# Two-layer encoder trunk on one core: first loads in another order, plain float32 behind three LayerNorms, gates at other points

## The chip, the cores and the metric

The kernel runs on 1 core of one Trainium2 chip. The metric is the device time of one execution in microseconds, median of the runs shown. Engines are named as in the profile: PE is TensorE (matmul), PEld its weight load, DVE is VectorE, ACT is ScalarE, POOL is GpSimd, SP is SyncE, which issues nearly all of this kernel's loads.

## The reference, cut to what matters

x is (1, 256, 1024) in float32; there are two layers, and LayerNorm sits behind every residual sum. The modulation of every sub-layer comes from one condition vector through a 1024 x 6144 matrix per layer.

```python
cond = jax.nn.silu(c)
for l in range(DEPTH):
    mod = (cond @ ada_w[l] + ada_b[l])[:, None, :]
    sh_m, sc_m, g_m, sh_f, sc_f, g_f = jnp.split(mod, 6, axis=-1)
    h = x * (1.0 + sc_m) + sh_m
    if l % 2 == 0:
        y = even_mixer(h, ...)            # pooling mixer | windowed attention, one in- and one out-projection
    else:
        y = spatial_gating_mixer(h, ...)  # gelu(h @ w_in) -> u, v; v normed, mixed over 128 positions; (u*v) @ w_out
    x = layer_norm(ALPHA * x + (1.0 + g_m) * y, ln_g[l, 0], ln_b[l, 0])
    h = x * (1.0 + sc_f) + sh_f
    if l % 2 == 0:
        y = swiglu(h, ...)                # 1024 -> 2816 -> 1024
    else:
        y = moe_swiglu(h, ...)            # router, top 2 of 8 experts, 1024 -> 3584 -> 1024 each
    x = layer_norm(ALPHA * x + (1.0 + g_f) * y, ln_g[l, 1], ln_b[l, 1])
```

The kernel works to float32 accuracy.

## The kernel before, in words

The 256 positions are two tiles of 128 (`t` = 0, 1); the 1024 channels are eight blocks of 128 (`KD`, index `kk`). Nothing is scheduled by a tool: each engine runs its instructions in the order in which the program writes them, and an instruction that waits holds up all behind it on its engine.

**Weights.** The class `Stream` (`st`) brings all weights in one fixed order, as pieces of 512 KB ("halves"), on the queue of SP, into a pool of 34 slots (`wtile`). `st.step()` takes the next half: a piece of the condition matrix goes through one DVE multiply-and-sum (`add_ada`, L270; the text calls it an ada step), a weight half is split into two reduced-float32 parts, `hi` by an ACT copy (L193) and `lo` by a DVE subtraction (L194), unless it is marked `RAW`. A split weight is multiplied by `mm3`: three reduced-float32 matmuls, hi x hh, lo x hh, hi x hl (L363 to L365), where `hh`, `hl` are the two parts of the activations. A RAW one is multiplied in plain float32. `st.advance(n)` takes n steps at that place in the program, `st.get()` takes steps until the halves asked for are there. `ROOM` is how many slots the loader leaves free.

**Start.** The condition vector (`cond`) and the small columns (`colt`) are loaded from ACT's queue, all else from SP's. For each `kk` in turn DVE does two ada steps (scale and shift) and `h` (L551), PE the in-projection in plain float32 (L561 to L571), and for the first four `kk` DVE makes one group of `band`, the pooling matrix (L513, L514). `cn` and the two `band` tiles take slots of the weights' pool.

**Attention.** `attend(0)` (tile 0: transposes L639, copies L641, matmuls L650), then `out_rows` (L717, plain float32, y = [pooled | attention] x w_out, 16 records of 128x512 per two `kk`), `attended` puts the heads' result behind (L664). DVE forms `o` (L656) between.

**Gates.** When all eight ada steps of a gate are made, `gate` puts it on all partitions by eight matmuls (L281) and two ACT copies; `st.finish` and `st.flush` say where.

**The three norms** (`norm_modulate`): DVE sums the residual and takes statistics, POOL the root, ACT (tile 0) or DVE (tile 1) normalises (`z`, L790, L797), PE transposes (L768), ACT or DVE apply scale and shift (`hf`), then `hh` and `hl` are made, and the first product behind the norm follows: gate and up of the first FFN block after norm 1 (`gu_tile`), `v` of the gating mixer after norm 2 (`v_half`), router logits and the dense first half of expert 0 after norm 3 (`logits`, `dense`).

**The rest**, FFN blocks, gating mixer and the experts, runs through `mm3` at one long stretch each.

Of the kernel before, what the change touches and what calls it, by code (L numbers as in the profile page):

```python
# [21 lines left out]
P = 128  # L22
# [29 lines left out]
def trunk_(es, tc, stream, experts, blocks, x, xT, c, columns, ada_w, ln_g, ln_b, ev_w_in, pool_w, ev_sink, ev_w_out,  # L52
# [51 lines left out]
    class Stream:  # L104
# [103 lines left out]
        def ensure(self, i):  # L208

            while self.made < i:  # L210
                self.step()
            self.flush()
# [21 lines left out]
        def get(self):  # L234
# [4 lines left out]
            for i in unit:  # L239
# [5 lines left out]
                if self.halves[i] == RAW:  # L245
                    for kk in range(part.shape[1]):
                        yield part[:, kk, :]
                    self.live -= 1
# [61 lines left out]
    for g in range(NFB // 2 + 1):  # L310
        if g < NFB // 2:
            for i, w in enumerate((ffn_w_gate, ffn_w_up)):
                st.add(cols(w[0], g * 256, 256))
                for _ in range(ADA[g]):
                    add_ada(*rest.pop(0))
# [3 lines left out]
    for nh in range(2):  # L319
        for k0 in (0, 4):  # L320
            st.add(cols(od_w_in[0], D + nh * 512, 512, k0, 4))
# [9 lines left out]
    def expert_units(stage, step):  # L331
# [111 lines left out]
    with ExitStack() as ph:  # L443
# [12 lines left out]
        A.dma_start(cond, c.to_broadcast([P, D]))  # L456
# [39 lines left out]
        cn = wtile(F32, "cn").rearrange("p (g n) -> p g n", g=4)  # L496
# [11 lines left out]
        band = [wtile(F32, "band").rearrange("p (g t n) -> p g t n", g=2, t=2) for _ in range(2)]  # L508

        def make_band(g):  # L510
            for t in range(NT):
                b = band[g // 2][:, g % 2, t, :]
# [27 lines left out]
        for t in range(NT):  # L540
            nc.sync.dma_start(xt[t], x[0, t * P:(t + 1) * P, :])
# [42 lines left out]
        st.ROOM = 15  # L584
# [109 lines left out]
        for g in range(4):  # L694
            psg.append(bank())
            for t in range(NT):
                T.matmul(psg[g][:, 0:S], lhsT=pt[:, t, g * P:(g + 1) * P], rhs=band[g // 2][:, g % 2, t, :],
# [11 lines left out]
        st.advance(2)  # L709
# [10 lines left out]
        o = [attend(0, V.tensor_copy, 1)]  # L720
# [16 lines left out]
        st.advance(4)  # L737
        out_rows(range(4, KD), (1,))

        def keep_warm(n):  # L740

            ps = psa.tile([P, 512], F32, tag="a", name="idle")
            for _ in range(n):
                T.matmul(ps[:, 0:P], lhsT=ones, rhs=ident, start=True, stop=True)

        def norm_modulate(y, gt, mods, then, keep=None, after=lambda: None):

            hh, hl = (big([P, KD, S], F32R, name=n) for n in ("hh", "hl"))  # L750
            then = then((hh, hl))
            z = [t4.tile([P, D], F32, tag="z", name="z", bufs=2) for _ in range(NT)]

# [17 lines left out]
            def affine(tp, t, q, eng):  # L771
                sa, sb = mods
                sl = slice(q * 4, q * 4 + 4), slice(t * P, (t + 1) * P)
                hf = keep[:, sl[0], sl[1]] if keep is not None else hp.tile([P, 4, P], F32, tag="hf", name="hf")
                for k in range(4):
                    kk = q * 4 + k
                    if eng is V:
                        V.tensor_scalar(hf[:, k, :], tp[:, k, :], sa[:, kk:kk + 1], sb[:, kk:kk + 1],
                                        op0=ALU.mult, op1=ALU.add)
                    else:  # L780
                        A.activation(hf[:, k, :], tp[:, k, :], AF.Identity, scale=sa[:, kk:kk + 1], bias=sb[:, kk:kk + 1])
                A.activation(hh[:, sl[0], sl[1]], hf, AF.Copy)
                return lambda: V.tensor_tensor(hl[:, sl[0], sl[1]], hf, hh[:, sl[0], sl[1]], op=ALU.subtract)
# [8 lines left out]
            lows = [affine(tp, 0, q, A) for q, tp in enumerate(tps)]  # L792
            next(then)
# [736 lines left out]
```

## Time and profile before

| what | value |
|---|---|
| time, median of 3 runs | 1343.64 us (1342.23 to 1344.15) |
| the profiled execution | 1340.86 us, span 1339.0 us |
| PE busy | 1284.6 us (96%) |
| DVE busy | 941.3 us (70%) |
| ACT busy | 679.3 us (51%) |
| DMA | 470.46 MB, mean 351 GB/s over the span |
| granted TensorE clock, mean | 0.982 of full speed |

Times inside the kernel are microseconds from the span's start. Idle time of PE stands in brackets in the rows of a timeline, with what it waited for. A plain float32 matmul shows as two records, a reduced-float32 one as one. Rows of a timeline merge like instructions in a row; a row's duration contains the tail of its last record, so the pace is better read from the start of a row to the start of the next.

### The profile page before, as it was taken

The numbers are of one execution on the slowest core, as the hardware profiler recorded it, in microseconds if no ns is written. First come the engines' busy times: TensorE is split into PE (matmuls) and PEld (weight loads), VectorE is DVE, ScalarE is ACT, GpSimd is POOL, SyncE is SP. The second block draws the span as 40 slices with busy tenths as digits, with TensorE's granted clock in tenths as the row PEclk, the third lists the DMA queues.
The fourth block names the chain that finished last, engine by engine and source line by source line (L and its number), as shares of the span: only waits on it lengthen the run. The fifth ranks groups of instructions, "written<-read, shape, count | busy, mean of one in ns | idle before, by whom it ended". The sixth has DMA issues, their size and how long they took to land. (4 is left out here: it accounts for less than half of the span.)

```text
span 1339.0 us, 19237 instructions
## 1 busy us (share of the span) xinstructions
PE 1284.6 (96%) x6468; PEld 945.1 (71%) x6468; DVE 941.3 (70%) x1162; ACT 679.3 (51%) x860; POOL 17.1 (1%) x73
## 2 busy tenths in 40 slices
PE   4987999998999999999999999999999999999995
PEld 3664999997888688644678888864467888886342
DVE  5696799986886888530798899753069899976303
ACT  0224444444625777421777777742167787774200
POOL 1001000000000000000000000000000000000001
PEclk9988999999999999999999999999999999999998
DMA  9995589997396589999999999899999999999993
GB/s 372 409 409 220 211 323 338 366 349 293 116 345 236 205 322 324 386 409 408 409 409 409 409 409 386 318 381 409 409 409 409 409 409 409 360 326 375 409 409 142
DMA packets 129579, 470.46 MB, mean 351 GB/s; under 512 B 14520, under 2 KB 14656, under 8 KB 129472
## 3 DMA queue, kind: packets, MB, share of 16 engines
q1 hardware_dynamic: 128880, 468.25, 90.7%
q8 instruction: 52, 0.85, 0.3%
q10 hardware_dynamic: 592, 0.91, 0.2%
q14 instruction: 55, 0.45, 0.1%
HBM read 468.05 MB, written 1.05 MB: 350 GB/s over the span
## 5 line engine op out<-in xcount | busy, mean ns | idle before, releaser
L194 DVE TENSOR_TENSOR lo<-raw,hi 128x1024 fp32r<-128x1024 f32 x506 | 604.5, 1220 | 118.0 <-ACT hi L193 93.4
L193 ACT ACTIVATE hi<-raw 128x1024 fp32r<-128x1024 f32 x506 | 514.9, 1054 | 147.0 <-PE y L364 17.0
L270 DVE CUSTOM_DVE_ANT_0 raw<-raw,cond,colt 128x1024 f32<-128x1024 f32 x96 | 118.5, 1278 | 0.0
L363 PE MATMUL pg<-hi,hh 128*128 128x512 f32 x288 | 117.3, 407 | 0.0
L364 PE MATMUL pg<-lo,hh 128*128 128x512 f32 x288 | 114.2, 397 | 0.7 <-DVE lo L194 0.7
L365 PE MATMUL pg<-hi,hl 128*128 128x512 f32 x288 | 114.0, 396 | 0.0
L364 PE MATMUL pu<-lo,hh 128*128 128x512 f32 x280 | 111.3, 397 | 1.2 <-DVE lo L194 1.2
L363 PE MATMUL y<-hi,ah 128*128 128x512 f32 x280 | 112.3, 401 | 0.0
L365 PE MATMUL y<-hi,al 128*128 128x512 f32 x280 | 111.0, 397 | 1.1 <-DVE al L1196 1.1
L363 PE MATMUL pu<-hi,hh 128*128 128x512 f32 x280 | 111.5, 398 | 0.0
L365 PE MATMUL pu<-hi,hl 128*128 128x512 f32 x280 | 111.0, 396 | 0.0
L364 PE MATMUL y<-lo,ah 128*128 128x512 f32 x280 | 110.9, 396 | 0.0
L1404 DVE TENSOR_TENSOR act<-act,pu 128x512 f32<-128x512 f32 (+1 forms) x47 | 31.2, 664 | 101.0 <-PE pu L1178 92.4
L1194 ACT ACTIVATE ah<-psT 128x512 fp32r<-128x512 f32 (+2 forms) x47 | 27.2, 578 | 132.6 <-PE psT L1189 132.2
L363 PE MATMUL psgu<-hh,hi 128*128 128x256 f32 x320 | 90.1, 282 | 0.0
L365 PE MATMUL psgu<-hh,lo 128*128 128x256 f32 x320 | 90.1, 281 | 0.0
L364 PE MATMUL psgu<-hl,hi 128*128 128x256 f32 x320 | 89.6, 280 | 0.0
L1178 PE MATMUL pu<-raw,hs 128*64 128x512 f32 (+1 forms) x384 | 76.6, 542 | 0.0
L1178 PE MATMUL pg<-raw,hs 128*64 128x512 f32 (+1 forms) x384 | 75.8, 542 | 0.0
L1402 ACT ACTIVATE act<-pg 128x512 f32<-128x512 f32 (+1 forms) x47 | 27.4, 584 | 84.1 <-PE pg L1178 62.3
L1210 PE MATMUL y<-raw,ah 128*64 128x512 f32 x288 | 65.5, 597 | 0.0
L363 PEld LDWEIGHTS pg<-hi,hh 128*128 128x128 f32 x288 | 54.2, 188 | 14.7 <-ACT hi L193 2.4
(281 smaller groups left out, 1872.2 us busy)
## 6 DMA issues: line engine op xcount, KB each, us to landing
raw<-in_experts SPq DMA_DIRECT2D x668, 512.0 KB, 10.1
raw<-in_stream SPq DMA_DIRECT2D x204, 512.0 KB, 7.3
lng<-in_ln_g SPq DMA_DIRECT2D x4, 512.0 KB, 6.7
lnb<-in_ln_b SPq DMA_DIRECT2D x4, 512.0 KB, 6.6
xT<-in_xT SPq DMA_DIRECT2D x2, 512.0 KB, 7.2
x<-in_x SPq DMA_DIRECT2D x2, 512.0 KB, 10.6
guest<-in_experts SPq DMA_DIRECT2D x2, 512.0 KB, 10.5
guests<-in_experts SPq DMA_DIRECT2D x2, 512.0 KB, 7.0
```

Of the source, the lines that this page charges most:

```text
L193: A.activation(hi, raw, AF.Copy)
L194: V.tensor_tensor(lo, raw, hi, op=ALU.subtract)
L270: V.tensor_tensor_reduce(raw[:, 0, :], raw[:, 0, :], cond, 1.0, adab[:, i:i + 1], ALU.mult, ALU.add, accum_out=mod[l, part][:, kk:kk + 1])
L363: T.matmul(ps, lhsT=l[0], rhs=r[0], start=start, stop=False)
L364: T.matmul(ps, lhsT=l[0], rhs=r[1], start=False, stop=False)
L365: T.matmul(ps, lhsT=l[1], rhs=r[0], start=False, stop=stop)
L1178: T.matmul(ps[rows_, 0:w.shape[-1]], lhsT=h[:, kk + k, :], rhs=w, start=kk + k == 0, stop=kk + k == KD - 1)
L1194: A.activation(ah[:, 0:n, :], ps[:, 0:n, :], AF.Copy)
L1210: T.matmul(y[n][rows_, :], lhsT=aT[0][:, kk, rows_], rhs=w[:, n * 512:(n + 1) * 512], start=fs[0] == 0 and kk == 0, stop=False)
L1402: A.activation(act[:, 0:n], pg[:, 0:n], AF.Silu)
L1404: V.tensor_tensor(act[:, 0:n], act[:, 0:n], pu[:, 0:n], op=ALU.mult)
```

## The change

1. Start: `cond` and `colt` are issued from SP's queue, ahead of everything else; `one_plus`, which waits for `colt`, stands on DVE behind the six distance operations instead of ahead of them; `cn` and `band` live in the pool `t8`, not in weight slots; the two loads of x stand 28 halves later in SP's queue; `ROOM` is 12 instead of 15.
2. Attention: no ada steps between the scores and `attend(0)` nor inside it; 14 ada steps behind it; the gate of the mixer (L281 before, L280 now) directly behind the second `attended`; the split of two halves of the second FFN block ahead of norm 1.
3. Norms: `use(t)` (the first product for tile t) directly behind that tile's scale and shift, in plain float32 from `hf`; `hh` and `hl` behind both tiles, not at all after norm 3; 12 weight halves become RAW; the idle matmuls between the logits (`keep_warm`) go.
4. `ensure` no longer flushes, so that the last gate's matmuls stand behind `dense(1)` instead of ahead of norm 3's transposes.

```diff
@@ -346,7 +345,7 @@
-                st.add_expert(r, unit[u * 2:u * 2 + 2])
+                st.add_expert(r, unit[u * 2:u * 2 + 2], RAW if (s, fs[0], stage) == (0, 0, 0) else what)
@@ -453,16 +452,13 @@
-        A.dma_start(cond, c.to_broadcast([P, D]))
+        nc.sync.dma_start(cond, c.to_broadcast([P, D]))
...
-        A.dma_start(colt, columns)
+        nc.sync.dma_start(colt, columns)
...
-        one_plus = adab.rearrange("p (h c) -> p h c", h=4)[:, :, 8:24]
-        V.tensor_scalar(one_plus, one_plus, 1.0, None, op0=ALU.add)
@@ -505,11 +501,14 @@
-        band = [wtile(F32, "band").rearrange("p (g t n) -> p g t n", g=2, t=2) for _ in range(2)]
+
+        one_plus = adab.rearrange("p (h c) -> p h c", h=4)[:, :, 8:24]
+        V.tensor_scalar(one_plus, one_plus, 1.0, None, op0=ALU.add)
+        band = t8.tile([P, 4, NT, S], F32, tag="b", name="band")
@@ -581,7 +578,9 @@
-        st.ROOM = 15
+        st.ROOM = 12
+        for t in range(NT):
+            nc.sync.dma_start(xt[t], x[0, t * P:(t + 1) * P, :])
@@ -706,7 +705,6 @@
         softmax_exp(1)
-        st.advance(2)
@@ -717,7 +715,8 @@
-        o = [attend(0, V.tensor_copy, 1)]
+        o = [attend(0, V.tensor_copy, 0)]
+        st.advance(4)
         ws.extend(st.get())
         out_rows((0,))
         attended(0, o[0])
@@ -727,29 +726,20 @@
             if kk == 1:
                 attended(1, o[1])
+                st.finish(2)
         for kk in range(4, KD):
             ws.extend(st.get())
-        st.advance(8)
+        st.advance(10)
         out_rows(range(4, KD), (0,))
-        st.finish(2)
         st.ends.pop(0)
         folded = fold(0, 3, 0, 0, "f0")
-        st.advance(4)
         out_rows(range(4, KD), (1,))
...
@@ -789,20 +774,22 @@
-            lows = [affine(tp, 0, q, A) for q, tp in enumerate(tps)]
-            next(then)
+            for q, tp in enumerate(tps):
+                affine(tp, 0, q, (A, A))
+            use(0)
             mu, rs = stats(1)
...
-            next(then, None)
-            after()
-            lows = [affine(tp, 1, q, (A, V)[q]) for q, tp in enumerate(tps)]
-            for fn in lows:
-                fn()
+            for q, tp in enumerate(tps):
+                affine(tp, 1, q, (A, V))
+            use(1)
+            if not split:
+                return z, None
+            hh, hl = (big([P, KD, S], F32R, name=n) for n in ("hh", "hl"))
+            for q in range(2):
+                hi_lo(hh[:, q * 4:q * 4 + 4, :], hl[:, q * 4:q * 4 + 4, :], hf[:, q * 4:q * 4 + 4, :])
...
-        def gu_tile(h, t):
+        def gu_tile(t):
             ps = psa.tile([P, 2, S], F32, tag="a", name="psgu")
-            for i in range(2):
-                for k, w in enumerate(ws[i]):
-                    mm3(ps[:, i, :], tile_of(h, k, t), w, k == 0 and i == 0, k == KD - 1 and i == 1)
-            return lambda: gu_act(t, ps)
+            for k in range(KD):
+                for i in range(2):
+                    T.matmul(ps[:, i, :], lhsT=hf[:, k, t * P:(t + 1) * P], rhs=ws[i][k], start=k == 0 and i == 0,
+                             stop=k == KD - 1 and i == 1)
+            gus.append(ps)
...
+        def tile_there(t):
+            if t == 0:
+                ws.extend(st.get())
+                dense(0, 0)
+                logits(0)
+            else:
+                logits(1)
+                dense(0, 1)
```

SP's queue at the start, before: the loads in order (`raw` are halves of the stream, `held` the pooling weights; `cond` and `colt` stand on ACT's queue and so not here).

```order
L530 DMA xT<-in_xT 128x1024
L157 DMA raw<-in_stream 128x1024 x10
L533 DMA xT<-in_xT 128x1024
L157 DMA raw<-in_stream 128x1024 x16
L539 DMA held<-in_pool_w 128x512
L541 DMA x_99<-in_x 128x1024
L541 DMA x_100<-in_x 128x1024
L157 DMA raw<-in_stream 128x1024 x68
```

The same place now:

```order
L455 DMA cond<-in_c 128x1024
L459 DMA colt<-in_columns 128x228
L529 DMA xT<-in_xT 128x1024
L157 DMA raw<-in_stream 128x1024 x10
L532 DMA xT<-in_xT 128x1024
L157 DMA raw<-in_stream 128x1024 x16
L538 DMA held<-in_pool_w 128x512
L157 DMA raw<-in_stream 128x1024 x28
L583 DMA x_99<-in_x 128x1024
L583 DMA x_100<-in_x 128x1024
L157 DMA raw<-in_stream 128x1024 x40
```

Two loads came to the head of the queue and the two of x went back by 28 halves.

DVE around `attend(0)`, before, from the last scaling of the pooled part (L707) on; an ISA pair is one ada step, `o` is the result of the heads of tile 0. Behind the last row eight ada steps stand ahead of the `sm` and `o` of tile 1.

```order
L707 TENSOR_SCALAR yT<-bank,colt 128x256 x4
L270 ISA raw,mod_79<-raw,cond,colt 128x1024
L270 ISA mod_79 128x1
L270 ISA raw,mod_79<-raw,cond,colt 128x1024
L270 ISA mod_79 128x1
L641 COPY prT<-tpp 128x512
L270 ISA raw,mod_79<-raw,cond,colt 128x1024
L270 ISA mod_79 128x1
L641 COPY prT<-tpp 128x512
```

The same place now; behind the last row 13 more ada steps follow, then `sm`, reciprocal and `o` of tile 1.

```order
L706 TENSOR_SCALAR yT<-bank,colt 128x256 x4
L640 COPY prT<-tpp 128x512 x4
L652 TENSOR_TENSOR sm<-sm,es__449 128x8
L653 RECIPROCAL sm<-sm 128x8
L655 TENSOR_TENSOR o<-po,sm 128x512
L269 ISA raw,mod_79<-raw,cond,colt 128x1024
L269 ISA mod_79 128x1
```

Six ada steps left the stretch ahead of the first `o`; 14 instead of eight stand between the two `o`.

PE from the last matmuls of `attend(1)` to the first product behind norm 1, before (96 rows of `psgu` in all, 48 of each tile):

```order
L650 MATMUL po<-held,prT 128x64 x8
L717 MATMUL y<-raw,yT 128x512 x4
L664 MATMUL tpo<-ident,o 128x128 x4
L717 MATMUL y<-raw,yT 128x512 x16
L281 MATMUL bank<-ident,mod_79 128x128 x8
L717 MATMUL y<-raw,yT 128x512 x8
L768 MATMUL tp<-ident,z 128x128 x16
L363 MATMUL psgu<-hi,hh 128x256
L364 MATMUL psgu<-lo,hh 128x256
L365 MATMUL psgu<-hi,hl 128x256
```

And now:

```order
L649 MATMUL po<-held,prT 128x64 x8
L715 MATMUL y<-raw,yT 128x512 x4
L663 MATMUL tpo<-ident,o 128x128 x4
L280 MATMUL bank<-ident,mod_79 128x128 x8
L715 MATMUL y<-raw,yT 128x512 x24
L758 MATMUL tp<-ident,z 128x128 x8
L807 MATMUL psgu<-raw,hf 128x256 x16
L758 MATMUL tp<-ident,z 128x128 x8
L807 MATMUL psgu<-raw,hf 128x256 x16
```

The gate moved ahead of 16 matmuls of `y`, and tile 0's product moved between the two sets of transposes, 16 plain matmuls in place of 48 reduced ones.

## Rows read from the trace of the kernel before

**Rows 1.** The page: busy time of PE; the DMA's total.

```profile
PE 1284.6 (96%) x6468; PEld 945.1 (71%) x6468; DVE 941.3 (70%) x1162; ACT 679.3 (51%) x860; POOL 17.1 (1%) x73
...
DMA packets 129579, 470.46 MB, mean 351 GB/s; under 512 B 14520, under 2 KB 14656, under 8 KB 129472
```

**Rows 2.** Busy time by stretch: from:to, length, engines, PE clock, DMA share, GB/s.

```profile
0.00:4.00 4.00, 0.00 (x0) 0.00 (x0) 0.17 (x2) 0.72 (x1) 2.88 (x25) 1.00 0.51 130
4.00:8.00 4.00, 0.00 (x0) 0.00 (x0) 0.00 (x0) 1.62 (x2) 1.42 (x27) 1.00 1.00 381
...
120.00:140.00 20.00, 13.38 (x82) 13.01 (x83) 13.94 (x27) 11.90 (x22) 4.03 (x10) 0.66 0.25 92
...
560.00:800.00 240.00, 239.15 (x1124) 159.87 (x1121) 158.24 (x159) 139.85 (x166) 0.00 (x0) 1.00 1.03 409
```

**Rows 3.** PE's waits: tile, for whom, us in total, times, longest.

```profile
PE tp L768 <- ACT z L790: 8.5, 3, 6.3
```

**Rows 4.** Timeline of DVE, 6 to 34 us: start, us, engine, what, [idle before].

```profile
8.20 0.20 DVE L465 TENSOR_SCALAR colt<-colt 128x64 f32<-128x64 f32 x1 [7.20 <-DMA colt<-in_columns]
...
28.41 0.43 DVE L513 SCALAR_TENSOR_TENSOR band<-consts,cn 128x256 f32<-128x256 f32 x1 [6.56 <-PE bank L566]
```

**Rows 5.** Timeline of PE, 0 to 60 us.

```profile
13.55 3.78 PE L561 MATMUL bank_y<-h,raw 128*128 128x256 f32 x8 [13.55 <-DVE h L551]
...
20.39 1.89 PE L561 MATMUL bank_y<-h,raw 128*128 128x256 f32 x8
22.11 1.88 PE L566 MATMUL bank<-raw,h 128*128 128x512 f32 x4
...
24.71 1.89 PE L561 MATMUL bank_y<-h,raw 128*128 128x256 f32 x8
...
32.74 3.78 PE L561 MATMUL bank_y<-h,raw 128*128 128x256 f32 x8 [3.54 <-DVE h L551]
...
57.60 1.13 PE L608 MATMUL bank<-attn,qall 64*128 64x256 f32 x8
```

**Rows 6.** Timeline of PE, 57 to 146 us.

```profile
68.83 1.07 PE L639 MATMUL tpp<-ident,scores 128*128 128x128 f32 x8
72.92 1.86 PE L650 MATMUL po<-held,prT 128*128 128x64 f32 x8 [3.03 <-DVE prT L641]
...
81.18 4.71 PE L717 MATMUL y<-raw,yT 128*128 128x512 f32 x8
...
95.80 0.60 PE L664 MATMUL tpo<-ident,o 128*128 128x128 f32 x4
96.23 13.90 PE L717 MATMUL y<-raw,yT 128*128 128x512 f32 x32
109.97 1.95 PE L281 MATMUL bank<-ident,mod 128*128 128x128 f32 x16
111.75 7.03 PE L717 MATMUL y<-raw,yT 128*128 128x512 f32 x16
125.04 1.97 PE L768 MATMUL tp<-ident,z 128*128 128x128 f32 x8 [6.26 <-ACT z L790]
```

**Rows 7.** DVE, 82 to 103 us: ada steps grouped (us in all, mean ns).

```profile
L270 DVE CUSTOM_DVE_ANT_0 raw<-raw,cond,colt 128x1024 f32<-128x1024 f32 x16 | 19.4, 1278 | 0.0
```

**Rows 8.** Timeline of DVE, 56 to 131 us: the splits ahead of norm 1.

```profile
113.53 4.63 DVE L194 TENSOR_TENSOR lo<-raw,hi 128x1024 fp32r<-128x1024 f32 x4 [10.21 <-ACT hi L193]
```

**Rows 9.** Timeline of ACT, 138 to 150 us: Silu of the two tiles of the product behind norm 1.

```profile
138.08 0.39 ACT L822 ACTIVATE gu<-psgu 128x256 f32<-128x256 f32 x1 [2.21 <-PE psgu L365]
...
143.74 0.39 ACT L822 ACTIVATE gu<-psgu 128x256 f32<-128x256 f32 x1 [0.46 <-PE psgu L365]
```

**Rows 10.** Timeline of PE: norm 2's second transposes; norm 3's gate and first transposes.

```profile
328.57 1.51 PE L768 MATMUL tp<-ident,z 128*128 128x128 f32 x8 [3.12 <-DVE z L797]
...
408.70 1.95 PE L281 MATMUL bank<-ident,mod 128*128 128x128 f32 x16
412.04 1.36 PE L768 MATMUL tp<-ident,z 128*128 128x128 f32 x8 [1.39 <-ACT z L790]
```

More of the change, by code (lines that the diff above doesn't have):

```diff
@@ L696, in trunk_ @@
             for t in range(NT):
-                T.matmul(psg[g][:, 0:S], lhsT=pt[:, t, g * P:(g + 1) * P], rhs=band[g // 2][:, g % 2, t, :],
+                T.matmul(psg[g][:, 0:S], lhsT=pt[:, t, g * P:(g + 1) * P], rhs=band[:, g, t, :],
                          start=t == 0, stop=t == NT - 1)
@@ L729, in trunk_, with norm_modulate @@
                 attended(1, o[1])
+                st.finish(2)
         for kk in range(4, KD):
             ws.extend(st.get())
-        st.advance(8)
+        st.advance(10)
         out_rows(range(4, KD), (0,))
-        st.finish(2)
         st.ends.pop(0)
         folded = fold(0, 3, 0, 0, "f0")
-        st.advance(4)
         out_rows(range(4, KD), (1,))
[L740 to L751, printed above, removed]
+        def norm_modulate(y, gt, mods, hf, use, split=True):
             z = [t4.tile([P, D], F32, tag="z", name="z", bufs=2) for _ in range(NT)]
+            sa, sb = mods
             def stats(t):
@@ L812, in trunk_ @@
         gu0 = t4.tile([P, NT, S], F32, tag="lnb", name="gu0", bufs=1)
-        def gu_tile(h, t):
+        hf = t8.tile([P, KD, S], F32, tag="a", name="hf")
+        ws = [list(st.get()) for _ in range(2)]
+        def gu_tile(t):
             ps = psa.tile([P, 2, S], F32, tag="a", name="psgu")
-            for i in range(2):
-                for k, w in enumerate(ws[i]):
-                    mm3(ps[:, i, :], tile_of(h, k, t), w, k == 0 and i == 0, k == KD - 1 and i == 1)
-            return lambda: gu_act(t, ps)
+            for k in range(KD):
[3 more added lines that the diff above has]
+            gus.append(ps)
         def gu_act(t, ps):
@@ L823, in gu_act @@
             V.tensor_tensor(gu0[:, t, :], gu0[:, t, :], ps[:, 1, :], op=ALU.mult)
-        def first_tile(h):
-            yield
-            ws.extend(list(st.get()) for _ in range(2))
-            ws.append(gu_tile(h, 0))
-        ws = []
-        z, h = norm_modulate(y, gates[0, 2], folded, first_tile, after=st.advance)
+        gus = []
+        z, h = norm_modulate(y, gates[0, 2], folded, hf, gu_tile)
         del st.AGE, st.ROOM
-        ws[2]()
         st.advance(4)
-        gu_tile(h, 1)()
+        for t in range(NT):
+            gu_act(t, gus[t])
         y = [[psy.tile([P, 512], F32, tag="y", name="y") for _ in range(2)] for _ in range(NT)]
@@ L905, in trunk_, with v_half @@
         ps2 = []
-        def v_half(h, t, ws):
+        hf = t8.tile([P, KD, S], F32, tag="b", name="hf")
+        ws = list(st.get()) + list(st.get())
+        def v_half(t):
             ps2.append(psa.tile([P, 512], F32, tag="a", name="psv"))
             for k, w in enumerate(ws):
-                mm3(ps2[t], tile_of(h, k, t), w, k == 0, k == KD - 1)
-        def first_tile(h):
-            yield
-            ws.extend(list(st.get()) + list(st.get()))
-            v_half(h, 0, ws)
-        ws = []
-        z, h = norm_modulate(y, gates[0, 5], (sa, sb), first_tile)
+                T.matmul(ps2[t], lhsT=hf[:, k, t * P:(t + 1) * P], rhs=w, start=k == 0, stop=k == KD - 1)
+        z, h = norm_modulate(y, gates[0, 5], (sa, sb), hf, v_half)
         st.AHEAD = 8
@@ L1007, in logits, with dense @@
                          start=k == 0, stop=k == KD - 1)
-                if warm:
-                    keep_warm(warm)
-        def dense(h, u, ws, ts=range(NT)):
-            for t in ts:
-                for k, w in enumerate(ws):
-                    kk = u * 4 + k
-                    mm3(pg0[t], tile_of(h, kk, t), w, kk == 0, kk == KD - 1)
-        def first_tile(h):
-            logits(0, 1)
-            st.guest(0)
-            yield
-            ws.extend(st.get())
-            dense(h, 0, ws, (0,))
-        ws = []
-        z, h = norm_modulate(y, gates[1, 2], (sa, sb), first_tile, hT)
+        def dense(u, t):
+            for kk in range(u * 4, u * 4 + 4):
+                T.matmul(pg0[t], lhsT=hT[:, kk, t * P:(t + 1) * P], rhs=ws[kk], start=kk == 0, stop=kk == KD - 1)
+        def tile_there(t):
[6 more added lines that the diff above has]
+                dense(0, 1)
+        z, _ = norm_modulate(y, gates[1, 2], (sa, sb), hT, tile_there, split=False)
         st.guest(2)
-        logits(1)
-        dense(h, 0, ws, (1,))
         lg = cst.tile([P, NT, NE], F32, name="lg")
@@ L1074, in trunk_ @@
         select(posm, 0, 0, oh0)
-        dense(h, 1, list(st.get()))
+        ws.extend(st.get())
+        for t in range(NT):
+            dense(1, t)
         st.flush()
```

34 lines of the change are left out of this document (12 added, 22 removed).

## Prediction

> **What bounds the kernel now.** The page comes first: PE is busy for 1284.6 us of a span of 1339.0, and the DMA moves 470.46 MB [rows 1]. Then the busy time by stretch, which shows where the missing 54 us lie: among the experts PE works 239.15 of 240 us although the DMA runs at 409 GB/s; from 120 to 140 us it works 13.38 of 20 at a clock of 0.66 [rows 2]. So PE sets the end nearly everywhere, and what can be won lies at the start, in the attention and around the norms. PE's list of waits gives 8.5 us to ACT's normalising ahead of three norms, 6.3 of it in one [rows 3]. [...] The sum below is made against the profiled execution (1340.86 us: its span and 1.9 around it); the median of the runs is 2.8 above it.
>
> **Start.** PE starts at 13.55, waiting for `h`; DVE had waited for `colt` until 8.20 [rows 4, 5], and six distance operations and two ada steps came behind. Now the distance operations fill that wait, and the ada steps start when their halves land. Up to the second half SP's queue has cond, colt, xT and two halves ahead, 2.2 MB; `cond` and `colt` delay the halves by nothing new, since they were part of what was moved in these first microseconds before, too. At 130 GB/s for 4 us and 381 from then on [rows 2] the second half is there at 4 + 1.69 / 0.381 = 8.4. An ada step and `h`, an estimated 1.9 with their hand-overs, give 10.3 for PE.
> The second gain is the stall at 28.41: `band`'s second tile waited 6.56 us for a weight slot that PE still read [rows 4], and PE then waited 3.54 at 32.74 [rows 5]. With `band` in another pool that is gone. A block of one `kk` takes 4.32 us at full clock (20.39 to 24.71), but the first took 20.39 - 13.55 = 6.84 at a low one [rows 5]. So PE goes from 10.3 through 6.84 + 7 x 4.32, plus 0.1 for the differently ordered last block, to 47.5 instead of 57.60: **-10.1**. A block needs 3.25 halves, 1.70 MB or 4.2 us at 409 GB/s, just under PE's 4.32: the last half of these lands at about 40.5, and its block starts at 43. If a block comes late once and costs the clock again, 7.5 is left; if the first halves land earlier, 12.
>
> **Attention.** Before, `attend(0)` went from 68.83 to 81.18, 12.35 us, with a wait of 3.03 for its first copy, behind two ada steps [rows 6]. Without ada steps between it should come near what `attend(1)` took, whose copies ran on an idle ACT: from 85.89 (81.18 + 4.71) to 92.3 (95.80 less eight records of 13.90 / 32 = 0.434 us), 6.4 with the heads' transposes [rows 6]. I take 6.8: -5.5. The first output rows took 4.71 instead of 8 x 0.434 = 3.5, at the low clock: -1.2.
> Against it stands a new wait. An ada step takes 19.4 / 16 = 1.21 us [rows 7]. Between the two `o` now stand 14, 16.9 us, instead of eight. From 47.5 on, `attend(0)` starts at 58.7 and ends at 65.5; `o` of tile 0 is done at 66.3, that of tile 1 at 66.3 + 16.9 + 1.1 = 84.3. PE is through two pieces of output rows and `attend(1)` by 65.5 + 3.5 + 0.4 + 6.1 + 3.5 = 79.0, and stands at the transposes of `o`, with the gate's matmuls and 24 instructions of `y` behind them in its queue: **+5.3**. Then its clock is low again, as behind the wait of 3.54; the first block's 6.84 - 4.32 prices that at +2.5. Behind it come 0.4, the gate's 1.8 and 6 x 3.48 for the rest of `y`: complete at 84.3 + 0.4 + 1.8 + 20.9 + 2.5 = 109.9, against 111.75 + 7.03 = 118.8 [rows 6]. Attention alone is **+1.1** (-4 if the wait hardly shows, +4 if the clock is lost for twice as long).
>
> **Norm 1.** Before, four splits on DVE, 113.53 to 118.16 [rows 8], stood ahead of the statistics; PE waited 6.26 us for `z` [rows 6] and the first product was ready at 138.08 (tile 0) and 143.74 (tile 1) [rows 9]. Now two splits stand there, done long before, and tile 0's `y` is complete 7 us ahead of tile 1's. Statistics, root and normalising took 118.16 to 125.04, 6.9 us, so tile 0's `z` comes about when PE ends `y`. Then: transposes and a first scale 1.4 (half of 1.97 [rows 6], and an estimated 0.4); tile 0's product, 32 records at (22.11 - 20.39) / 8 = 0.215 [rows 5], 6.9; tile 1's transposes and scale 1.4, its own chain of 6.9 running beside tile 0's product; tile 1's product 6.9. That is 16.6, to 126.5 against 143.74, and beyond the 8.9 already there **-8.3** (4 if PE waits long enough to lose its clock, 10 if the second transposes are hidden better).
> In plain float32 the product itself is dearer: 6.9 us against 143.74 - 138.08 = 5.66 per tile [rows 9], a factor of 1.22. [...]
>
> **Norms 2 and 3.** In norm 2 PE waited 3.12 us for the second transposes [rows 10]; tile 0's product now covers that chain: -3.1. The low clock behind it, between 0 and the 2.5 above, is taken as -1.2; two tiles of 16 records at 0.434 instead of 1.22 times less are +2.5; the scale of tile 1 is +0.4. **-1.4** (+1 to -3). In norm 3 the gate's 1.95 us and a wait of 1.39 go from ahead of the transposes [rows 10], -3.3; the gate comes back behind `dense(1)`, +1.8; four dense pieces of eight records grow by 0.6 each, +2.5; eight idle matmuls go, -1.8 by the gate's eight of the same shape; the gather waits for the gate's ACT copies, +0.5, a third of the 1.39 in which they stood. **-0.3** (+2 to -3).
>
> **At nothing:** 12 halves less to split (1.16 us of DVE each by [rows 8]), since DVE and ACT are off the path once the norms are passed; the two loads of x, 28 halves or 36 us later at about 79, wanted near 103; `ROOM`, as long as loads wait for slots. The FFN, the mixer and the experts run their unchanged instructions earlier.
>
> **Sum.** -10.1 + 1.1 - 8.3 - 1.4 - 0.3 = -19.0: 1321.9 for the profiled execution, 1324.6 for the median, rounded to 1325.
>
> **The rivals.**
> *The clock stays low (slower).* The new products stand between transposes on PE, and the idle matmuls are gone. [...] For it: the 0.66 between 120 and 140 us, around the transposes of norm 1 [rows 2, 6]. [...] Against: after 13.55 plain float32 alone brought the clock back, the second block taking 4.32 [rows 5], and few waits are left around the products. Chance 0.05, and 0.02 for other losses larger than the gain.
> *PE still waits in norm 1.* Tile 0's `z` is ready within some half us of PE's need by my sum, and two splits, the last ada steps or POOL's root may push it back. 2 us late with the clock lost (2.5), once per tile, takes 7 to 8 off: 1332. Chance 0.15.
> *The shift is absorbed (no change).* At 409 GB/s for 240 us among the experts [rows 2], PE could meet halves that can't come sooner: 1341 to 1344. Against: 470 MB at 409 GB/s are 1150 us of 1339, and the DMA's share of 0.25 from 120 to 140 us [rows 1, 2] is that of a queue that waits for slots. Chance 0.05.
>
> **How the numbers follow.** The sum has 0.73, with its own range of 1317 to 1331 by the bounds; with the rival in norm 1, 0.88 is faster. 0.05 is no change, within 0.2% (2.7 us, about what a measurement of this kernel can tell from none), 0.07 slower. Leaving out the last two and the ends of the others, the range of 8 in 10 is 1315 to 1334.
>
> **What would show it.** Right: PE's first matmul near 10.3 and the scores near 47.5; no wait at `band`; PE idle about 5 us ahead of a transpose of `o`, ended by DVE; no long wait at norm 1's transposes; the second Silu near 127; the experts earlier by the whole sum. Wrong: PE waiting for halves in the first 48 us; a longer wait for `o`; a low clock through the plain products; waits for loads after 560.

## The result, and the profile after

The changed kernel takes 1323.78 us (median of 4 runs, 1322.54 to 1327.66) against 1343.89 for the one before: a ratio of 0.9856 [0.9832, 0.9881]. The forecast was 1325, and 20.1 us lie between the medians, where the sum had 19.0. The profiled execution of the changed kernel has a span of 1323.2 us, 15.8 less than the profiled one of before. The two differences are not the same because executions of one kernel lie some us apart, for a reason that the experiments come to.

The page of the changed kernel, its busy time and the granted clock in 40 slices, answers to [rows 1]:

```profile
span 1323.2 us, 19021 instructions
...
PE 1281.8 (97%) x6388; PEld 928.4 (70%) x6388; DVE 926.6 (70%) x1142; ACT 665.0 (50%) x840; POOL 16.6 (1%) x73
...
PEclk9999999999999999999999999999999999999997
```

PE has about as much work as before (1281.8 us against 1284.6), in a shorter span: of the 15.8 us, 13.0 are idle time that went. Where it went is in PE's list of waits of the changed kernel (us in total, times, longest), beside [rows 3]:

```profile
PE bank_y L558 <- DVE h L548: 11.4, 1, 11.4
PE tpo L663 <- DVE o L655: 5.5, 1, 5.5
...
PE tp L758 <- ACT z L775: 0.7, 1, 0.7
PE psg L1080 <- ACT gt L282: 0.7, 1, 0.7
```

The transposes `tp` ahead of the three norms' products wait 0.7 us for ACT's `z` instead of 8.5, and no longer for DVE's, for which they had waited another 4.7 (2 times, the longest 3.1). A new wait of 5.5 stands at `tpo`, the transposes of `o`. PE's timeline of the changed kernel (start, duration, operation, count, and in brackets the idle time ahead and what ended it) shows the places:

```profile
11.40 3.78 PE L558 MATMUL bank_y<-h,raw 128*128 128x256 f32 x8 [11.40 <-DVE h L548]
...
48.55 1.14 PE L607 MATMUL bank<-attn,qall 64*128 64x256 f32 x8
...
84.97 1.11 PE L663 MATMUL tpo<-ident,o 128*128 128x128 f32 x4 [5.54 <-DVE o L655]
85.87 2.93 PE L280 MATMUL bank<-ident,mod 128*128 128x128 f32 x16
88.64 20.77 PE L715 MATMUL y<-raw,yT 128*128 128x512 f32 x48
109.24 1.04 PE L758 MATMUL tp<-ident,z 128*128 128x128 f32 x8
110.39 7.17 PE L807 MATMUL psgu<-raw,hf 128*128 128x256 f32 x32
117.40 1.04 PE L758 MATMUL tp<-ident,z 128*128 128x128 f32 x8
118.55 7.17 PE L807 MATMUL psgu<-raw,hf 128*128 128x256 f32 x32
125.37 0.47 PE L362 MATMUL psgu<-hh,hi 128*128 128x256 f32 x1
...
388.10 1.04 PE L758 MATMUL tp<-ident,z 128*128 128x128 f32 x8
389.24 3.70 PE L995 MATMUL pg<-raw,hT 128*128 128x512 f32 x8
392.78 1.85 PE L989 MATMUL pslg<-colt,hT 128*128 128x8 f32 x16
394.48 1.07 PE L758 MATMUL tp<-ident,z 128*128 128x128 f32 x8
395.67 3.11 PE L989 MATMUL pslg<-colt,hT 128*128 128x8 f32 x16
398.63 5.33 PE L995 MATMUL pg<-raw,hT 128*128 128x512 f32 x8
```

Norm 1 is now one unbroken row from 109.24 to 125.37. In norm 3 (the last six rows) `pg`, dense pieces of the same shape, take 3.70 us once and 5.33 once. By milestones of the two timelines, each row the difference to the kernel before (us):

| stretch, to | forecast | measured | all so far |
|---|---|---|---|
| start, to the scores (57.60 -> 48.55) | -10.1 | -9.05 | -9.05 |
| attention, to `y` complete (118.8 -> 109.4) | +1.1 | -0.35 | -9.4 |
| norm 1, to behind its product (143.53 -> 125.37) | -8.3 | -8.8 | -18.2 |
| FFN, to norm 2's transposes (324.08 -> 306.85) | 0 | +0.9 | -17.2 |
| norm 2, to behind its product | -1.4 | -2.2 | -19.4 |
| mixer, to `y`'s end (408.70 -> 388.10) | 0 | -1.2 | -20.6 |
| norm 3, to the gather (432.42 -> 414.41) | -0.3 | +2.6 | -18.0 |
| 47 expert blocks, to the last product (1317.64 -> 1300.55) | 0 | +0.9 | -17.1 |
| last product, to the end | 0 | +1.3 | -15.8 |

### The profile page after: what moved, and what is told of

Its sections match the earlier page's. It is cut to its first block, busy times and chain, and to the rows that moved or that the text cites. A ratio compares the mean times of both kernels' runs of the same rounds, so it can differ in the third digit from the quotient of the medians.

```text
span 1323.2 us, 19021 instructions
## 1 busy us (share of the span) xinstructions
PE 1281.8 (97%) x6388; PEld 928.4 (70%) x6388; DVE 926.6 (70%) x1142; ACT 665.0 (50%) x840; POOL 16.6 (1%) x73
## 3 DMA queue, kind: packets, MB, share of 16 engines
HBM read 468.05 MB, written 1.05 MB: 355 GB/s over the span
## 5 line engine op out<-in xcount | busy, mean ns | idle before, releaser
L194 DVE TENSOR_TENSOR lo<-raw,hi 128x1024 fp32r<-128x1024 f32 x494 | 590.8, 1222 | 107.1 <-ACT hi L193 80.8
L193 ACT ACTIVATE hi<-raw 128x1024 fp32r<-128x1024 f32 x494 | 503.3, 1055 | 146.7 <-PE psgu L363 20.2
L362 PE MATMUL pg<-hi,hh 128*128 128x512 f32 x272 | 110.7, 407 | 0.0
L363 PE MATMUL pg<-lo,hh 128*128 128x512 f32 x272 | 107.9, 397 | 0.7 <-DVE lo L194 0.7
L364 PE MATMUL pg<-hi,hl 128*128 128x512 f32 x272 | 107.6, 396 | 0.0
L363 PEld LDWEIGHTS pu<-lo,hh 128*128 128x128 f32 x280 | 52.7, 188 | 14.9 <-DVE lo L194 2.0
## 6 DMA issues: line engine op xcount, KB each, us to landing
raw<-in_experts SPq DMA_DIRECT2D x668, 512.0 KB, 10.1
guest<-in_experts SPq DMA_DIRECT2D x2, 512.0 KB, 10.1
```

What stands on the lines that cost most here:

```text
L193: A.activation(hi, raw, AF.Copy)
L194: V.tensor_tensor(lo, raw, hi, op=ALU.subtract)
L362: T.matmul(ps, lhsT=l[0], rhs=r[0], start=start, stop=False)
L363: T.matmul(ps, lhsT=l[0], rhs=r[1], start=False, stop=False)
L364: T.matmul(ps, lhsT=l[1], rhs=r[0], start=False, stop=stop)
```

## The experiments

Every edit is made on the changed kernel. Its profiled execution, 1324.94 us, is the one that single runs stand beside; the places in the timelines tell more than the totals.

**e1: band back in the pool of weight slots.**
```
-cn = t8.tile([P, 4, S], F32, tag="a", name="cn")
+cn = wtile(F32, "cn").rearrange("p (g n) -> p g n", g=4)
```
and `band` in two weight tiles as before.

> The changed kernel with cn and the two band tiles back in the weights' slots; queue and DVE order stay as changed. Theory (the stall at band's second tile was worth about two thirds of the gain at the start): DVE waits some 6.5 us for a matmul of the in-projection before a band row, PE waits about 3.5 us and loses its clock, and the scores start at 48.55 + 3.5 + 2.5 to 3.2 = 54.6 to 55.3. Rival (the slots matter little now, because the loads are 3 us ahead): scores at 48.6 to 50. Whole time, theory: about 6 us over the changed kernel.

It took 1331.92. DVE and PE of this run, each in its timeline:

```profile
26.48 0.42 DVE L512 SCALAR_TENSOR_TENSOR band<-consts,cn 128x256 f32<-128x256 f32 x1 [5.63 <-PE bank L563]
...
30.81 3.78 PE L558 MATMUL bank_y<-h,raw 128*128 128x256 f32 x8 [3.54 <-DVE h L548]
```

The stall of [rows 4] is back (5.63 us for 6.56), the wait of [rows 5] with the same 3.54, and the records behind it run at a low clock (3.78 us for eight instead of 1.89, as at 32.74 in the kernel before, where the granted clock was 0.50 from 33 to 37 us). The scores come 7.07 us later (55.62), 0.32 of it because PE began at 11.72, and the loss is carried unchanged to norm 1 (7.04) and to the gather (7.04). So nearly 7 of the 9 us of the start are the place of `cn` and `band`.

**e2: `cond` and `colt` on ACT's queue** (`A.dma_start` instead of `nc.sync.dma_start`), the other loads as they are.

> The changed kernel with cond and colt issued from ACT's queue again; the order on DVE stays as changed. Theory (the gain of 2.15 us at PE's first matmul comes from DVE's order, the distance operations ahead of the wait, and the first ada step waits for its half whichever queue carries cond): PE's first matmul at 11.4 within 0.5, scores at 48.6 within 0.5. Rival (the queue is what counts): colt lands near 8 as before, the first ada step no earlier than 8.5, PE's first matmul at 11.6 or later; a second rival is that xT and the halves, now at the head of SP's queue, land earlier and PE starts at 10.3, as the prediction had it.

It took 1324.74. `colt` landed later, at 8.12 instead of 5.68, but PE began at 11.26 and the scores at 47.95. An ada step needs `cond`, `colt` and a half. The first one begins at 8.26 here, right behind `colt` and with no wait for its half; in the changed kernel it begins at 8.33, behind a wait of 2.45 us for the half. Both come at about the same time, so the queue is worth nothing measurable here.

**e3: `o` of both tiles ahead of the ada steps**
```
-o.append(attend(1, A.copy, 2))
+o.append(attend(1, A.copy, 0))
...
-st.advance(10)
+st.advance(18)
```

> The changed kernel without ada steps inside the second attend: o of tile 1 is formed behind six ada steps instead of 14, the eight others come behind it, so that 16 ada steps and two splits stand between it and norm 1's statistics. Theory (the 5.54 us wait at the transposes of o and the low clock behind it cost 8 us, but DVE's work ahead of norm 1 stays the same and becomes the bound there): no wait at those transposes, y complete at 101.4, statistics only from about 98.8, norm 1's first transposes at about 105.5 after a wait of some 4 to 6 us, first matmul behind its product near 124, so at most 1 to 2 us of the 8 stay. Rival (the wait is pure loss): norm 1's transposes at 101.4 and the matmul behind its product at 117.4, 8 us earlier.

It took 1324.97, no change. The wait for `o` is gone (the transposes stand at 78.54 without one) and `y` is complete 8 us earlier, at 101.5. But in PE's timeline of this run norm 1 waits:

```profile
104.75 1.97 PE L758 MATMUL tp<-ident,z 128*128 128x128 f32 x8 [3.22 <-ACT z L775]
106.51 1.98 PE L807 MATMUL psgu<-raw,hf 128*128 128x256 f32 x4
```

DVE has the same ada steps to do and now does them ahead of the statistics. With the wait and the slower pace behind it (tile 0's product takes 8.92 us, 106.51 to 115.43, instead of 7.01), norm 1's product is done 2.0 us earlier (123.41), not 8.

**e4: tile 0's product behind tile 1's transposes**, in all three norms: `use(0)` moved behind `tps = [transposed(1, q) for q in range(2)]`. The plain float32 stays.

> The changed kernel with tile 0's product behind the transposes of tile 1 in all three norms, still in plain float32. Theory (the gain around the norms comes from tile 0's product covering tile 1's chain): PE waits again for tile 1's z, about 3.3 us in norm 1 and 2 to 3 in norm 2 and 3, each with a low clock behind it; the matmul behind norm 1's product moves from 125.37 by 3.3 + 2.5 to about 131, the whole time by 10 to 15 us. Rival (the gain comes from plain float32 not needing the split activations and from the splits ahead of the statistics being gone): the whole time moves by less than 5 us.

It took 1333.94. In PE's timeline, norm 1:

```profile
109.91 1.04 PE L758 MATMUL tp<-ident,z 128*128 128x128 f32 x8
114.06 1.94 PE L758 MATMUL tp<-ident,z 128*128 128x128 f32 x8 [3.11 <-DVE z L782]
```

The wait is back three times (3.11, 3.25, 3.10). Norm 1 takes 20.2 us instead of 16.1, norm 2 20.4 instead of 16.0, norm 3 27.8 instead of 26.3. So the gain at the norms is the order, tile 0's product under tile 1's normalising; the plain float32 by itself costs time (7.01 us a tile against 5.66 before). Whether split halves in the same order would have won as much was not run.

**e5: norm 3's gate back ahead of its transposes** (`self.flush()` in `ensure`).

> The changed kernel with the last gate's matmuls ahead of norm 3's transposes again. Counted from norm 2's first transposes, the changed kernel has norm 3's first transposes 81.25 us later and the gather 107.56 later. Theory (the prediction's: the gate and ACT's copies ahead of z cost 3.3 there, and 1.8 + 0.7 come back when it stands behind the dense pieces, so moving it gained about 0.8): transposes at 84.6, gather at 108.3. Rival (the place of the gate also decides where the clock falls, since its 16 full records stand between the thin ones): low clock behind the logits gone, gather at 105.5, that is, moving the gate lost 2.

It took 1324.3. The transposes wait 1.39 us again, as in [rows 10], and from `y`'s end to the gather it takes 27.92 instead of 26.31: moving the gate did not cause norm 3's loss. Of the 1.61 us, only 0.70 is the gate itself (3.34 us with its wait ahead of the transposes, 2.64 with the gather's wait behind the dense pieces, about the 0.8 expected). Most of the rest is that the clock fell sooner here (0.52 at 400 to 404 us): tile 1's logits took 3.69 us instead of 3.11 and the dense piece behind them 5.60 instead of 5.33.

**e6: one idle matmul behind each of tile 0's logits matmuls**, as the kernel before had them.

> The changed kernel with one idle matmul of 128x128 behind each logits matmul of tile 0, as before. [...] Theory (that stretch of thin matmuls lets the clock fall, and the idle matmuls held it): logits of tile 1 take 1.85 instead of 3.11, dense 3.70 instead of 5.33, so 2.9 are saved and 1.9 paid for the idle matmuls; gather 106.6 behind norm 2's first transposes instead of 107.56. Rival (the fall has to do with the missing split work or with the time since norm 2, not with thin matmuls): still low behind the logits, gather at 109.4.

It took 1321.99. The clock is 1.00 through norm 3, and tile 1's first dense piece takes 3.68 instead of 5.33. Tile 1's logits take 3.06 as before (3.11), so it isn't the clock that sets them. From norm 2 to the gather nothing is won (107.70 against 107.56): the eight idle matmuls cost what the clock gives back. What does set the logits is seen on ACT and DVE, here in the timeline of the changed kernel:

```profile
395.15 0.46 ACT L768 ACTIVATE hT<-tp,f1sb,f1sa 128x128 f32<-128x128 f32 x1 [3.52 <-PE tp L758]
396.09 0.81 ACT L768 ACTIVATE hT<-tp,f1sb,f1sa 128x128 f32<-128x128 f32 x2 [0.48 <-DVE hT L766]
397.38 0.46 ACT L768 ACTIVATE hT<-tp,f1sb,f1sa 128x128 f32<-128x128 f32 x1 [0.48 <-DVE hT L766]
...
395.65 0.41 DVE L766 TENSOR_SCALAR hT<-tp,f1sa,f1sb 128x128 f32<-128x128 f32 x1 [3.10 <-ACT hT L768]
396.59 0.76 DVE L766 TENSOR_SCALAR hT<-tp,f1sa,f1sb 128x128 f32<-128x128 f32 x2 [0.53 <-ACT hT L768]
397.87 0.41 DVE L766 TENSOR_SCALAR hT<-tp,f1sa,f1sb 128x128 f32<-128x128 f32 x1 [0.53 <-ACT hT L768]
```

The scale of tile 1 is shared out between ACT and DVE piece by piece, but each waits for the other (0.48 to 0.53 us): eight pieces one behind the other take 3.1 us, no less than the 2.90 that ACT alone takes for tile 0, and the logits, 1.85 us of matmuls, follow them. In the kernel before, ACT and DVE took one half of the same scale each, and there they ran side by side, from 417.83 to 419.64 us. The lines are ACT's, DVE's and, for the logits, PE's timeline before:

```profile
417.83 1.51 ACT L781 ACTIVATE hT<-tp,f1sb,f1sa 128x128 f32<-128x128 f32 x4 [0.87 <-PE tp L768]
418.27 1.37 DVE L778 TENSOR_SCALAR hT<-tp,f1sa,f1sb 128x128 f32<-128x128 f32 x4 [0.58 <-PE tp L768]
417.19 1.04 PE L768 MATMUL tp<-ident,z 128*128 128x128 f32 x8
420.87 1.84 PE L1006 MATMUL pslg<-colt,hT 128*128 128x8 f32 x16
```

Both engines wrote `hT` then too, so that alone does not make them take turns. What the change made new is that they alternate, and read from the same `tp` instead of one each. The one place in the six rows where they overlap is where they pass from the first `tp` to the second (ACT's row of two to 396.90, DVE's from 396.59); that speaks for the shared `tp`, but no run tests it. And before, a dense piece stood between tile 1's transposes and its logits and covered the scale. The change moved it ahead of tile 0's logits.

**e7: dense pieces between the logits**, so that work covers the scale: logits of tile 0, a dense piece, the transposes, a dense piece, logits of tile 1, the others.

> The changed kernel with the dense pieces between the thin ones: logits of tile 0, dense piece of tile 0, transposes of tile 1, dense piece of tile 1, logits of tile 1, third dense piece, positions, fourth dense piece; no instruction more. Two splits go behind the choice of experts. Theory (the clock falls behind thin matmuls in a row): full clock through norm 3, 2.9 us saved, gather at 104.7 behind norm 2's first transposes instead of 107.56, if the routing chain on DVE (2.6 us to the mask, some 5.7 from the positions to the gather) stays hidden behind a dense piece of 3.5 and one more with the gate (5.4). Rival: the chain shows, PE waits for mask or for the chosen rows by 1 to 3 us, and the gather comes at 106 to 108.

It took 1328.4. Tile 1's logits take 1.85 now: the cover works. But tile 0's logits, which now follow their transposes directly, wait for the scale in their place: they took 2.87, beside ACT's eight pieces of 2.90 in all (394.30 to 397.20). The clock fell earlier too (0.64 from 398 to 402), and the dense piece behind took 5.33. From the transposes to the gather it is 26.14 against 26.31: the uncovered scale and the low clock moved to tile 0, and next to nothing is won. The total is worse for a fall in the mixer (4.7 us), where nothing was edited.

**e8: e3 with DVE's work moved too.** Norm 1's statistics of tile 0 go ahead of the last four ada steps, and two more steps stand behind tile 1's normalising:
```
-o.append(attend(1, A.copy, 2))
+o.append(attend(1, A.copy, 0))
...
-st.advance(10)
+st.advance(12)
...
+def early_steps():
+    st.advance(4)
+    ws.extend(list(st.get()) for _ in range(2))
...
+early=early_steps, mid=lambda: st.advance(2)
```

> As the kernel with o first (no ada steps inside the second attend), but norm 1's statistics of tile 0 stand ahead of the last four ada steps, and the two splits behind tile 1's normalising. Theory (in that kernel DVE's 16 ada steps and two splits ahead of the statistics made the new wait of 3.22 us; DVE has enough time if the statistics come first): no wait over 1 us at the transposes of o or of norm 1; y complete near 101, norm 1's first transposes at 100.8 to 102.5, psT transposes behind its product at 120.5 to 122.5 instead of 129.13. Rival (DVE is short of time in sum, whatever the order): the wait appears at tile 0's scale, which needs the last ada steps, or at tile 1's, and psT stays at 125 to 127.

It took 1322.93. Norm 1 waits 0.84 us in all, and up to norm 2 6.3 us are won (300.54 instead of 306.85). At norm 3 all of it is gone. Windows over the mixer in this run (length; busy time and count of PE, PEld, DVE, ACT, POOL; granted clock; DMA share; GB/s):

```profile
350.00:355.00 5.00, 5.00 (x29) 3.96 (x28) 5.00 (x7) 0.60 (x1) 0.00 (x0) 0.93 1.01 384
355.00:360.00 5.00, 5.00 (x17) 3.71 (x16) 3.61 (x6) 1.26 (x2) 0.00 (x0) 0.50 0.99 382
360.00:365.00 5.00, 5.00 (x16) 3.97 (x16) 2.55 (x4) 0.79 (x2) 0.00 (x0) 0.50 0.84 341
```

PE is busy throughout and waits for nothing, and yet its granted clock is 0.50 from 355 to 365 us. The fall comes among the mixer's four groups (350.92 to 363.73): each has four records of bias matmuls, whose operand has 8 rows, then eight records of 128 rows. The edit doesn't touch them.

**e9: the changed kernel again**, unedited.

> The changed kernel unchanged, beside the next two, to see how far its single executions spread and what its clock does between norm 2 and norm 3. The mixer has there four times four matmuls that contract over 8 rows only (the bias of the spatial mix) and four times eight plain ones of 128x128. [...] Theory (a stretch of thin matmuls there lets the clock fall in some executions and not in others): single times spread over 4 to 7 us, with the mean clock going along. Rival (the spread comes from the end of the kernel or from loads): times do not follow the clock.

Median 1327.05 of 6 runs (1322.40 to 1329.26), ratio 0.9883 [0.9860, 0.9906]. The times follow the mean granted clock: 1322.40 at 0.995, 1324.14 at 0.991, 1326.54 and 1327.55 at 0.990, 1329.12 and 1329.26 at 0.988. In the profiled one of them the clock is 0.83 from 362 to 372 us, from the last of the mixer's groups on; in the first profile it was 1.00 there. So 7 us lie between executions of the same instructions, and single runs can't decide over less.

**e10: the bias matmul with 128 rows**, 120 of them zero, as the only edit.
```
-bs = cst.tile([8, P], F32, name="bs")
+bs = cst.tile([P, P], F32, name="bs")
+G.memset(bs, 0.0)
...
-lhsT=ident[0:8, g + i:g + i + 1].to_broadcast([8, P])
+lhsT=ident[:, g + i:g + i + 1].to_broadcast([P, P])
```

> The changed kernel with the mixer's 16 bias matmuls contracting over 128 rows (the bias padded with zeros) instead of 8: the same result, the same columns, the same time at equal clock. Theory (the few rows in use are what lets the clock fall there): no low clock between 350 and 380 us in the profile, single times closer together than the changed kernel's and their slowest below 1325. Rival (the short plain matmuls around them, or something else, let it fall): as the changed kernel, the same spread, median within 1 us.

1323.35 (1321.53 to 1324.58, 4 runs), ratio 0.9855 [0.9832, 0.9878], against 0.9883 for e9 on the same chip; the intervals overlap. In its profile the mixer ran at 1.00. The timelines of the changed kernel and of e10 show the price of a group:

```profile
362.57 1.16 PE L953 MATMUL pssv<-wsT,vn 128*128 128x128 f32 x8
363.66 1.12 PE L949 MATMUL pssv<-bs,ident 8*128 8x256 f32 x4
364.72 1.16 PE L953 MATMUL pssv<-wsT,vn 128*128 128x128 f32 x8
```
```profile
361.99 1.05 PE L954 MATMUL pssv<-wsT,vn 128*128 128x128 f32 x8
362.88 1.03 PE L950 MATMUL pssv<-bs,ident 128*128 128x256 f32 x4
363.75 1.05 PE L954 MATMUL pssv<-wsT,vn 128*128 128x128 f32 x8
```

From one group to the next it takes 1.76 us (361.99 to 363.75) instead of 2.15, although 16 times as many rows are multiplied. Norm 3's clock still falls (0.79 from 394 to 400 us, 0.50 from 400 to 404).

**e11: e8 and e10 together.**

> The balanced order (o first, statistics of tile 0 ahead of the last four ada steps, two splits behind tile 1's normalising) with the mixer's bias matmuls over 128 rows. In the balanced kernel norm 2's first transposes came 6.3 us earlier, at 300.54, and the mixer then lost just that to a low clock. Theory (the two have nothing to do with each other): with full rows the mixer keeps its clock, norm 3's transposes come near 381.8, and the time is 1317 to 1319, 5 to 7 us below the changed kernel. Rival (what comes early is lost again by norm 3, to loads that cannot come sooner or to the clock): 1322 to 1325.

1314.87 (1313.09 to 1316.62, 5 runs), ratio 0.9797 [0.9777, 0.9818], clear of both e9 and e10. The windows of e8, in this run:

```profile
350.00:355.00 5.00, 5.00 (x37) 4.72 (x36) 5.00 (x7) 0.25 (x1) 0.00 (x0) 1.00 0.99 363
355.00:360.00 5.00, 5.00 (x26) 3.89 (x25) 3.43 (x6) 1.40 (x3) 0.00 (x0) 1.00 1.01 401
360.00:365.00 5.00, 5.00 (x23) 4.08 (x22) 3.77 (x6) 3.02 (x4) 0.00 (x0) 1.00 1.03 416
```

In this profile, with the wide bias, the clock holds, and what was won up to norm 2 (7.68 us, 299.17 instead of 306.85) arrives at the gather with 1.1 more from the shorter groups (405.63 instead of 414.41).

**e12: e11 with 108 columns in the logits' matmuls** instead of 8. The product of the other 100 columns is not used.
```
-rhs=wr[:, k, :]
+rhs=colt[:, 64 + k * NE:172 + k * NE]
```

> The balanced kernel with full rows, whose logits matmuls of norm 3 now stream 108 columns instead of 8 (the logits are the last eight of them; the others are columns that are there anyway and are thrown away). [...] A matmul of 128x8 took about as long as one of 128x128 there. Theory (few columns, like few rows, are what lets the clock fall): no low clock in norm 3, the gather 24.0 behind norm 3's first transposes instead of 26.3, and a median of 1312 to 1313 against 1314.87. Rival (the transposes, or something that no width of the logits changes): low clock as before, gather at 26.3 to 28, median 1314 to 1316.

1313.74 (1311.69 to 1314.88, 5 runs), ratio 0.9788 [0.9771, 0.9806]: the fastest here, though not to be told from e11 by its time. The profile tells them apart. Norm 3's clock in e11 and then in e12, windows:

```profile
388.00:392.00 4.00, 3.88 (x15) 2.49 (x16) 2.79 (x13) 1.52 (x3) 0.00 (x0) 0.73 1.03 419
392.00:396.00 4.00, 4.00 (x16) 2.10 (x14) 2.73 (x7) 2.48 (x3) 0.00 (x0) 0.84 0.83 333
```
```profile
388.00:392.00 4.00, 3.97 (x19) 2.77 (x20) 2.34 (x9) 2.21 (x4) 0.00 (x0) 1.00 1.03 422
392.00:396.00 4.00, 4.00 (x19) 2.32 (x18) 3.73 (x13) 2.56 (x3) 0.00 (x0) 1.00 1.02 409
```

From the transposes to the gather e12 takes 24.65 us, e11 26.32: the 1.67 are what the low clock had cost. Tile 0's logits take 1.77 from their start to the transposes (1.70 with 8 columns). Those of tile 1 take 3.14 (3.06 with 8), since they wait for the scale either way.

## Why the prediction was right, and where its terms were off

The places and the causes of the gain were right, and the size of most terms. That the median came within 1.2 us of the forecast is luck in part: the profiled pair differs by 15.8 us, not by 19.0, the misses of single stretches run from -1.45 to +2.9 and partly cancel, and e9's median of the same kernel is 3.3 us longer.

**Start: the mechanism right, 1.05 too much.** The sum let one ada step stand behind the second half. DVE's timeline of the changed kernel shows what did:

```profile
5.68 0.20 DVE L506 TENSOR_SCALAR colt<-colt 128x64 f32<-128x64 f32 x1 [1.71 <-DMA colt<-in_columns]
8.33 1.28 DVE L269 CUSTOM_DVE_ANT_0 raw<-raw,cond,colt 128x1024 f32<-128x1024 f32 x1 [2.45 <-DMA raw<-in_stream]
...
9.60 1.28 DVE L269 CUSTOM_DVE_ANT_0 raw<-raw,cond,colt 128x1024 f32<-128x1024 f32 x1
```

The first half itself landed only at 8.33, about when the second was forecast, so both steps came behind, and PE began at 11.40, not 10.3. The second step, `h` and the hand-overs took 1.80 (9.60 to 11.40) for the estimated 1.9. From there to the scores it took 37.15 us, the 37.2 of the sum, and no later half was late. The first block is slow again, 6.80 us (11.40 to 18.20) against 4.32 for the next; that this is a low clock is read from the pace alone, the granted clock of the profile being 1.00 there before and now.

**Attention: +1.1 measured as -0.35.** The new wait was sized right (5.54 for 5.3). `attend(0)` took 6.24 instead of the 6.8 taken, and the clock behind the wait (0.60 granted from 84.97 to 88.64) cost 1.5, not 2.5: from `tpo` to `y` it took 88.64 - 84.97 = 3.67 against 0.43 + 1.78 at full clock.

**Norm 1: -8.3 measured as -8.8.** 16.13 us instead of 16.6, with neither wait. The plain product takes 7.01 us a tile (110.39 to 117.40) against 5.66, a factor of 1.24, for which the sum had 1.22.

**Norm 2 and the mixer: 2 us more than forecast.** In norm 2 (-2.2 for -1.4) the wait of 3.12 us is gone as said. The 0.4 for tile 1's scale did not come: from the second transposes to the product it is 1.16 us before (328.57 to 329.73) and now (315.08 to 316.24). The mixer's -1.2 is no gain of the change: about 1.6 us of low clock (0.61 granted) fell at 384 to 388 us of the profiled execution of before, and in this one of after the mixer ran at 1.00. e9 shows that such a fall comes and goes.

**FFN: +0.9 had no term.** Its first transposes `psT` wait 0.57 us for DVE's `gu`, which now stands behind two ada steps and two splits: it begins at 128.66, 3.3 us behind the product, where it began 0.9 behind (144.45) before.

**Norm 3: the step that failed.** The term -0.3 became +2.6, beyond its own bound of +2. Its known parts were about right: gate and wait -3.34, gate and the gather's wait back +2.64 (2.3), dense pieces +2.6 (2.5), idle matmuls -2.24 (1.8). Two were missing. The sum put tile 1's logits directly behind their transposes at no price, though the dense piece that had covered the scale was gone from there and the scale's pieces now alternate between the engines: the logits wait for it (+1.25). And it counted the idle matmuls as a pure saving, though without them the clock falls behind the logits (0.63 from 398 to 400 us, 0.51 from 400 to 402; +1.65). e6 and e12 show both apart: the clock comes back and the logits stay at 3.1; e7 shows that a dense piece in between takes tile 1's logits back to 1.85.

**The experts and the end.** The shift goes through the 47 blocks almost whole, -17.9 at the first and -17.6 at the last: the rival in which the loads absorb it is out. The last product took 6.56 us instead of 5.32 at a granted clock of 0.50 to 0.69, +1.2. With the start, the FFN, norm 3 and the experts, that is more than the other stretches won beyond the forecast, and so the profiled pair differs by 15.8 and not by 19.0.

**The other rivals.** *The clock stays low* was wrong where it stood. Norm 1's and norm 2's products ran at 1.00, and the eight transposes between them too (1.04 us each time): here transposes with plain products on both sides cost no clock. A low clock did come, small and elsewhere, behind matmuls of 8 columns (0.51 from 400 to 402 us) or 8 rows (0.83 from 362 to 372 us in e9), and in the mixer it was there before the change as well (0.61 from 384 to 388 us). *PE still waits in norm 1* did not happen (no wait), but e3 shows how near it is: with `y` 8 us earlier DVE is late, and the wait is 3.22.

**What stays open.** For norm 3 it is shown that the bare logits let the clock fall: the dense piece behind them took 5.29 to 6.73 us in all eleven profiles that have them (the changed kernel and every run but e6 and e12), 3.68 and 3.62 in e6 and e12. Whether it is their few columns or their shortness was not separated, and the fall in the last product was not tried. For the mixer it is likely and not shown. e10 alone is not shown faster than the changed kernel, and that the wide bias holds the clock rests on e8 against e11, one profile each, and on e11's clock in its runs (0.993 to 0.996, against 0.988 to 0.995 in e9). Over all profiles the clock fell in the mixer in six of the eleven with 8 rows (before, e3, e4, e7, e8, e9) and in none of the three with 128 (e10, e11, e12). Three are few, where five of eleven kept their clock anyway.

## What to carry to other kernels

To remove a wait, move the work that the other engine has ahead of its next due result as well: ordering `o` first alone gave 8 us at one place and took 6 back at the next (e3), and with DVE's statistics moved the gain held up to norm 2 (e8). A product that is dearer by a factor of 1.24 can pay, if half of the work then starts before the other half is ready (e4). When a piece of work moves, ask what it had covered at its old place (norm 3). Read several executions before you believe a difference below the spread of one kernel's times, and look at the granted clock by stretch first.

## What the runs showed of the hardware that was not expected

PE's granted clock was 0.50 over 10 us in which it was busy for all 10.00 (e8, 355 to 365). Such a fall in the mixer came in some executions and not in others of the same instructions (0.83 from 362 to 372 us in e9, 1.00 in the first profile of the changed kernel), and it cost from nothing up to the 6.3 us of e8. Padding the matmuls at such a place from 8 to 128 rows, or from 8 to 108 columns, went with a clock of 1.00 there in the profiles of e11 and e12, and cost next to nothing: a group of the mixer even fell from 2.15 to 1.76 us, and tile 1's logits took 3.14 instead of 3.06. Two engines that shared out the scaling of one tile piece by piece took turns, 0.46 and 0.41 us a piece, and were no faster than one alone (3.1 against 2.90 us); by halves, in the kernel before, they ran side by side (417.83 to 419.64 us).
